# Second expert stage: sums kept in four banks over all experts, rows gathered per expert in float32, two more places for weights

## The chip, the cores and the metric

One Trainium2 chip, one of its cores. The metric is the device time of one execution in microseconds (us); lower is better. The kernel before was timed three times: 2516.45, 2519.05 and 2519.34 us, median 2519.05 us.

## What is computed

The program runs two transformer blocks of two layers each on 256 rows of 1024 floats. Each layer of the second block ends in a stage of 16 experts. In the first such stage two streams of 256 rows go through it (x and a context stream); in the second, which is the end of the program but for a last norm, only x does. What one stage computes, from the reference (`h` is the normalised and modulated x, `n` = 256, so each expert takes `cap` = 32 rows):

```python
def ec_moe(h, w_r, w1, w3, w2):
    cap = max(1, EC_CAPACITY * n // N_EXPERTS)
    aff = jax.nn.softmax((h @ w_r).astype(jnp.float32), axis=-1)
    gate, idx = lax.top_k(jnp.swapaxes(aff, 1, 2), cap)
    xin = jax.vmap(lambda hb, ib: hb[ib])(h, idx)
    hid = jax.nn.silu(jnp.einsum('becd,edf->becf', xin, w1)) * jnp.einsum('becd,edf->becf', xin, w3)
    ye = jnp.einsum('becf,efd->becd', hid, w2) * gate[..., None].astype(h.dtype)
    return jax.vmap(lambda yb, ib: jnp.zeros((n, D), h.dtype).at[ib.reshape(-1)].add(yb.reshape(-1, D)))(ye, idx)
...
        h2 = modulate(rmsnorm(x, g_norm2[i]), sh2, sc2)
        x = x + gt2 * ec_moe(h2, w_router[i], w_e1[i], w_e3[i], w_e2[i])
```

Every expert has three weight matrices of 1024 x 1024 floats (4 MiB each), so a stage reads 192 MiB.

## The kernel before

**The weights.** All large weights come through `Ring.load` and `Ring.load_pairs` (L137, L144): one DMA of 1 MiB on SP's queue into a tile of 8 KiB per partition. Such a tile is called a *place* here, and such a DMA a *load*. The ring hands the places out in a fixed order, so a load waits until the work that last used its place is done, and SP issues its DMAs strictly in order: a load that waits holds up all behind it. In the second expert stage, `moe(1, ...)`, the ring has 21 places (L1569 to L1572): two that are free from early on (`early`), one in `late`, the memory of the second half of the attention's normalised rows (`hp[1]`) at the ninth position, and 17 places `rE1_0` to `rE1_16` that lie where the attention stage had its own tiles and come free one by one as that stage ends. The memory of the first half of those normalised rows (`hp[0]`) is not a place: it takes the pieces that are gathered from. A stage makes 192 loads. One expert needs 12: four steps of the first product (`first_product`, L1610) with one load of `w_e1` and one of `w_e3` each, and four loads of `w_e2` for the second product.

**The start of the stage.** After the router's top-k (`topk`, L969) VectorE has the 16 x 32 row numbers. `u_onehot` (L989) spreads them over 128 partitions with one product on `ones16` and compares them with the row numbers, which gives the one-hot matrix `G` for all 16 experts (2 x 512 columns). `u_pieces` (L1005) splits the scaled rows into a high and a low float32r half (`hTh`, `hTl`), ScalarE writing one and VectorE the other. `u_gather` (L1039) then makes, for each of the eight blocks of 128 model columns, four products of 512 columns, and ScalarE or VectorE writes the result for all 16 experts at once into `xin` (16 KiB per partition), with the norm's scale and shift. Two blocks at a time are gathered ahead of each of the four steps of expert 0's first product (L1639 to L1648). Up to there the order of the instructions is as written (`tc.manual_schedule` from L1491 until `tail.close()`, L1650); behind it a scheduler sets the order on each engine.

**The loop over experts** (L1847 to L1855). Step e makes two steps of the first product of expert e, the whole `second_product` of expert e - 1, and the other two steps. `second_product` (L1783) turns the gated values (`gated`, L1774, into a tile `hd`) by four transposes, multiplies with `w_e2` into two banks `y`, scales by gate and output gate into `yg`, splits into `yh` and `yl` (`evac_hl`, L395) and sends the 32 rows back to their places among 256 by products with the one-hot `Se` (L1838, L1839), each 128 x 256 result in a bank of its own `b`; VectorE adds each to x (L1841).

PSUM has eight banks, all handed out by `bank` (L82). `gate_rows` (L538) prepares the output gate `gt` by two products of 512 columns (L543).

Of the kernel before, what the change touches and what calls it, by code (L numbers as in the profile page):

```python
# [69 lines left out]
def model(ctx, tc, I, out):  # L70
# [810 lines left out]
    RT = {}  # L881
# [107 lines left out]
    def u_onehot(s, bd, G):  # L989

        st = {}

        def spread():
            ixf = RT[s][1]
            d = bd()[0:16, 0:512].rearrange("p (e c) -> p e c", c=32)
            dve.tensor_tensor(d, ixf[:, None, :].to_broadcast([16, 16, 32]), ident[:16, :16, None].to_broadcast([16, 16, 32]),
                              op=ALU.mult)
            st["b"] = bank("b")
            pe.matmul(st["b"], ones16, d.rearrange("p e c -> p (e c)"), start=True, stop=True)

        def rows(t):
            return lambda: dve.tensor_scalar(G[:, t], st["b"], tokid[:, t:t + 1], None, op0=ALU.is_equal)
        return [spread, rows(0), rows(1)]
# [555 lines left out]
    def moe(l, ss, hp, sh, r, tail, ctx=None):  # L1559
# [3 lines left out]
        with ExitStack() as st:  # L1563
            if ns == 2:
                ring = Ring(st, f"rE{l}", 15, 0, [8, 9, 10, 11, 12, 13, 14, 0, 3, 1, 2, 4, 5, 6, 7])
                ring.ps.append(hp[1])
                ring.ps[0:0] = early
            else:
                ring = Ring(st, f"rE{l}", 17, 0, [0, 1, 2, 3, 4, 12, 13, 6, 5, 7, 8, 10, 9, 11, 14, 15, 16])  # L1569
                ring.ps[0:0] = [late]  # L1570
                ring.ps[6:6] = [hp[1]]
                ring.ps[0:0] = early  # L1572
            mo = opool(st, "mo", reuse_waits="tile")
            G = ns
            xin = mo.tile([128, 16 // G, 8, G, ns, 32], F32, name="xin")
            rg = mo.tile([128, 32], F32, name="rg")

# [5 lines left out]
            rp = opool(rst, "rt", reuse_waits="tile", side="right")  # L1583
# [25 lines left out]

            def first_product(hb, e, i):  # L1610
                if ns == 2:
                    return first_products(hb, e, i)
                t1, t3 = ld(I["w_e1_2"][l, e], i), ld(I["w_e3_2"][l, e], i)
                for kk in range(2):
                    k = 2 * i + kk
                    lhs = xin[:, e, k, 0, 0]
# [6 lines left out]
            xs, px, pl = u_pieces(0, r, hp)  # L1623
            xs["to"] = lambda c: xin[:, :, c, :, 0]
            gx, ex = u_gather(l, 0, xs, (dve, act))
            hb0 = [bank("h") for _ in range(4 if ns == 2 else 1)]
            if ns == 2:
# [3 lines left out]
            run(px[:2])  # L1631
            if ns == 2:
                run([ec[4], gc[6], ec[5], gc[7], ec[6], ec[7]])
            xs["G"] = (ctx["gp"] if ctx else rp).tile([128, 2, 512], F32R, name="G", tag="G")
            oh = u_onehot(0, lambda: per.tile([128, 512], F32R, name="bd", tag="mt", bufs=1), xs["G"])
            run([oh[0], pl[0], oh[1], pl[1], oh[2]])
            if ns == 2:
                sel(1)
            run([gx[0], gx[1], ex[0], ex[1]])  # L1639
            first_product(hb0, 0, 0)  # L1640
            run([gx[2], gx[3], ex[2], ex[3]])
            run(px[2:])
            run(pl[2:])
            first_product(hb0, 0, 1)
            run([gx[4], gx[5], ex[4], ex[5]])
            first_product(hb0, 0, 2)
            run([gx[6], gx[7], ex[6], ex[7]])
            first_product(hb0, 0, 3)  # L1648
# [15 lines left out]
            sh.close()  # L1664
            ap = opool(st, "ex", reuse_waits="tile")
            gt = ap.tile([128, D], F32, name="gt")

# [106 lines left out]
            def gated(e, hb):  # L1774

                hd = ap.tile([128, 512 * ns], F32, name="hd", tag="hd")
# [6 lines left out]
            def second_product(e, hd):  # L1783
# [59 lines left out]
            gate_rows(ap, gt, l, 1, rowsel, (lambda: per.tile([128, 512], F32, name="sel", tag="mt", bufs=1)) if ns == 2 else None)  # L1843
            if ns == 2:
                return pairs(hb0)
            hd = gated(0, hb0)
            for e in range(1, 16):  # L1847
# [3 lines left out]
                second_product(e - 1, hd)  # L1851
                first_product(hb, e, 2)
# [12 lines left out]
    moe(1, [0], hp, sh, r, tail)  # L1865
    sh1.close()
# [36 lines left out]
```

## Time and profile before

| what | us |
|---|---|
| three runs, median | 2519.05 |
| the profiled execution, its device time | 2521.02 |
| the profiled execution, its span (first to last instruction) | 2519.3 |
| TensorE busy, share of the span | 2365.8, 94% |
| chain that ended last: TensorE / DMA | 67% / 25% |
| mean granted TensorE clock | 0.987 of full |

The profiled execution took 2521.02 us, 1.97 above the median of the three runs; its span leaves out 1.7 us around the first and last instruction. The stage in question fills the end of the span, from about 2060 us on. In the page's forty slices the DMA's share is at nine tenths or more in the last slices and TensorE's digit falls to 7 and 8 there, while in the rest of the span it is the other way round. All times below are positions in this span.

### The profile page before, as it was taken

Reading aid. Unit: us, or ns where it says so; the run is one execution under the profiler, and the core shown is the slowest. Engines: PE = TensorE matmul, PEld = TensorE weight load, DVE = VectorE, ACT = ScalarE, POOL = GpSimd, SP = SyncE. Lnnn points to the kernel's source line nnn. Section 1 sums busy time; section 2 is a strip of 40 time slices with the busy share of each in tenths; the row PEclk is TensorE's granted clock in tenths of the full one; section 3 lists DMA queues with packets and bytes.
Section 4 is the critical chain, followed back from the end, with each engine's and each line's share of the span. In section 5 each row is a group of like instructions: output and inputs, shape, how many; then the busy total and the mean of one; then the engine's idle time right before and its main releaser. Section 6 shows DMA issues by size and latency. Waiting matters only on the chain.

```text
span 2519.3 us, 38429 instructions
## 1 busy us (share of the span) xinstructions
PE 2365.8 (94%) x15004; PEld 1709.6 (68%) x15004; DVE 1387.0 (55%) x2819; ACT 1062.8 (42%) x2152; POOL 134.4 (5%) x188
## 2 busy tenths in 40 slices
PE   8999999999999999999999999998999989778776
PEld 7788979788999999789843443447879973222222
DVE  5687665686867777987721111225688763222223
ACT  5765555465757656565420000005656532000001
POOL 0100000010000000100300000001010000000000
PEclk9999999999999999999999999998999989999999
DMA  7577565467654444746689999997674679999998
GB/s 272 217 258 261 184 218 175 160 243 272 215 150 152 163 168 168 220 151 231 245 359 427 427 426 427 427 416 248 189 232 148 226 307 398 427 426 427 427 427 347
DMA packets 274935, 709.11 MB, mean 281 GB/s; under 512 B 27135, under 2 KB 181489, under 8 KB 220994
## 3 DMA queue, kind: packets, MB, share of 16 engines
q1 hardware_dynamic: 274754, 706.66, 73.9%
q8 instruction: 118, 1.93, 0.3%
q14 instruction: 63, 0.52, 0.1%
HBM read 705.50 MB, written 1.12 MB: 280 GB/s over the span
## 4 chain that ended last, share of the span: by engine, by line
PE 67%; DMA 25%; DVE 5%; ACT 1%; issue 1%; POOL 0%; DVEq 0%; POOLq 0%; SPq 0%; ACTq 0%
DMA w<-in_w_e_dram 24%; PE b L86 13%; PE b L88 13%; PE b L87 13%; PE h L1607 5%; PE acc L86 3%; PE acc L87 3%; PE acc L88 3%; PE b L509 1%; PE b L1191 1%; PE y L1710 1%; DVE wl L161 1%; PE b L1048 1%; DMA w<-in_w_ada_dram 1%; PE o L1311 1%
## 5 line engine op out<-in xcount | busy, mean ns | idle before, releaser
L161 DVE TENSOR_TENSOR wl<-w,wh 128x512 fp32r<-128x512 f32 x896 | 600.8, 696 | 191.8 <-ACT wh L159 153.7
L159 ACT ACTIVATE wh<-w 128x512 fp32r<-128x512 f32 x896 | 531.6, 627 | 225.9 <-PE b L87 114.2
L86 PE MATMUL b<-hTh,wh 128*128 128x256 f32 x1584 | 453.6, 287 | 3.3 <-ACT hTh L386 2.1
L87 PE MATMUL b<-hTl,wh 128*128 128x256 f32 x1584 | 448.0, 283 | 2.2 <-DVE hTl L377 1.4
L88 PE MATMUL b<-hTh,wl 128*128 128x256 f32 x1584 | 448.4, 283 | 0.0
L86 PEld LDWEIGHTS b<-hTh,wh 128*128 128x128 f32 x1584 | 300.5, 190 | 15.5 <-issue 5.7
L87 PEld LDWEIGHTS b<-hTl,wh 128*128 128x128 f32 x1584 | 299.5, 189 | 5.2 <-DVE hTl L377 1.8
L88 PEld LDWEIGHTS b<-hTh,wl 128*128 128x128 f32 x1584 | 300.0, 189 | 0.3 <-DVE wl L161 0.3
L1607 PE MATMUL h<-w,xin 128*64 128x512 f32 x1024 | 255.9, 597 | 1.7 <-DMA w<-in_w_e_dram 1.7
L396 ACT ACTIVATE yh<-yg 128x256 fp32r<-128x256 f32 x96 | 39.1, 417 | 454.5 <-DVE yg L1831 267.8
L1607 PEld LDWEIGHTS h<-w,xin 128*64 128x64 f32 x1024 | 88.5, 137 | 146.0 <-issue 132.6
L1620 PE MATMUL h<-w,xin 128*32 128x512 f32 x512 | 163.3, 610 | 8.2 <-DMA w<-in_w_e_dram 7.1
L1831 DVE SCALAR_TENSOR_TENSOR yg<-y,rg,gt 128x256 f32<-128x256 f32 x64 | 28.1, 478 | 250.0 <-PE y L1800 249.8
L88 PE MATMUL b<-hT,wl 128*128 128x256 f32 x560 | 156.5, 279 | 0.2 <-DVE wl L161 0.2
L86 PE MATMUL b<-hT,wh 128*128 128x256 f32 x560 | 156.6, 280 | 0.1
L87 PE MATMUL b<-hT,wh 128*128 128x256 f32 x560 | 156.3, 279 | 0.0
L1800 PE MATMUL y<-w,hT 128*32 128x512 f32 (+1 forms) x544 | 129.9, 585 | 26.6 <-DMA w<-in_w_e_dram 26.2
L1621 PE MATMUL h<-w,xin 128*32 128x512 f32 x512 | 123.7, 610 | 21.9 <-DMA w<-in_w_e_dram 21.9
L1710 PE MATMUL y<-w,xin 128*64 128x512 f32 x448 | 111.6, 598 | 5.6 <-DMA w<-in_w_e_dram 5.6
L1800 PEld LDWEIGHTS y<-w,hT 128*32 128x32 f32 x544 | 30.3, 111 | 123.8 <-issue 68.8
L88 PEld LDWEIGHTS b<-hT,wl 128*128 128x128 f32 x560 | 105.2, 188 | 0.4 <-DVE wl L161 0.4
L86 PEld LDWEIGHTS b<-hT,wh 128*128 128x128 f32 x560 | 105.2, 188 | 0.3 <-ACT wh L159 0.3
(395 smaller groups left out, 4110.6 us busy)
## 6 DMA issues: line engine op xcount, KB each, us to landing
w<-in_w_e_dram SPq DMA_DIRECT2D x384, 1024.0 KB
w<-in_w_in_dram SPq DMA_DIRECT2D x92, 1024.0 KB
w<-in_w_ada_dram SPq DMA_DIRECT2D x48, 1024.0 KB
w<-in_ffn_w_up_dram SPq DMA_DIRECT2D x44, 1024.0 KB
w<-in_ffn_w_down_dram SPq DMA_DIRECT2D x22, 1024.0 KB
w<-in_dil_w_qkv_dram SPq DMA_DIRECT2D x18, 1024.0 KB
w<-in_w_branch_dram SPq DMA_DIRECT2D x18, 1024.0 KB
w<-in_sb_w_qkv_dram SPq DMA_DIRECT2D x12, 1024.0 KB
```

The costliest lines, as they stand in the source:

```text
L86: pe.matmul(o, s[0], m[0], start=start, stop=False, skip_group_check=True)
L87: pe.matmul(o, s[0], m[1], start=False, stop=False, skip_group_check=True)
L88: pe.matmul(o, s[1], m[0], start=False, stop=stop, skip_group_check=True)
L159: act.activation(hi, part, AF.Copy)
L161: dve.tensor_tensor(lo, part, hi.bitcast(F32), op=ALU.subtract)
L396: act.activation(hi, src, AF.Copy)
L1607: pe.matmul(hb[2 * j + n][64 * q:64 * q + 64], xin[:, p, k, q].rearrange("p s c -> p (s c)"), ts[j][q][:, kk, n * 512:n * 512 + 512], star ...
L1620: pe.matmul(hb[0][32 * n:32 * n + 32], lhs, t1[:, kk, ns_], **fl)
L1621: pe.matmul(hb[0][64 + 32 * n:96 + 32 * n], lhs, t3[:, kk, ns_], **fl)
L1710: pe.matmul(yb[p][cols.start // 512][64 * q:64 * q + 64, cols.start % 512:(cols.stop - 1) % 512 + 1], xin[:, p, k, :].rearrange("p q s c - ...
L1800: pe.matmul(yb[cols.start // 512][M * q:M * q + M, cols.start % 512:(cols.stop - 1) % 512 + 1], hT[:, k], w, start=kk == 0, stop=last, ski ...
L1831: dve.scalar_tensor_tensor(yg[:, c_], yb[n][:, c_], rg[:, 16 + e:17 + e], gt[:, xs_], op0=ALU.mult, op1=ALU.mult)
```

## The change

Only the second expert stage (`ns == 1`) is changed; up to its first instruction the order on every engine is the same as before.

- The rows are no longer scaled, split and gathered for all experts at once. `u_onehot` multiplies the comparison by the rows' norm factor as it writes the one-hot `G1` in float32, first for experts 0 and 1 (64 columns), later for the other 14 (448 columns). A new `taken(e, c)` makes, for one expert and one block c of model columns, two float32 products with 32 columns (the unchanged rows `xr` stationary, `G1` moving) into 32 columns of one bank, which ScalarE or VectorE moves into `xe` with scale and shift. Expert e + 1 is taken while expert e is worked on.
- The results are summed in four banks `acc` over all 16 experts, set to zero at the start by four products of 512 columns; x gets them after the last expert alone. The 120 additions to x of experts 0 to 14 go.
- `xin` goes (16 KiB), as does `hd` (now `gtr[0]`); `G1` and `xe` come. With that one more place `rE1_17` fits, and `hp[0]`, now unused in the stage, becomes a place too: 23 in place of 21, the new one `hpr` at the ninth position and `rE1_17` at the end.
- The small tiles of the start (`sel16`) lie on the other side of memory.

```diff
+        def spread(es=slice(0, 16)):
+            def f():
+                ixf, n = RT[s][1], es.stop - es.start
...
+                pe.matmul(st["b"][:, cs], ones16, st["d"][:, cs], start=True, stop=True, skip_group_check=True)
...
+                    dve.tensor_scalar(G[:, t, cs], st["b"][:, cs], tokid[:, t:t + 1], r[t], op0=ALU.is_equal, op1=ALU.mult)
...
+            return [u(slice(a, b)) for a, b in ((0, 2), (2, 16)) for u in (spread, lambda es: rows(0, es), lambda es: rows(1, es))]
...
-                ring = Ring(st, f"rE{l}", 17, 0, [0, 1, 2, 3, 4, 12, 13, 6, 5, 7, 8, 10, 9, 11, 14, 15, 16])
+                sh.close()
+                hp = (opool(sh, "hpr", reuse_waits="tile", side="right"), hp[1])
+                ring = Ring(st, f"rE{l}", 18, 0, [0, 1, 2, 3, 4, 12, 13, 6, 5, 7, 8, 10, 9, 11, 14, 15, 16, 17])
                 ring.ps[0:0] = [late]
-                ring.ps[6:6] = [hp[1]]
+                ring.ps[6:6] = [hp[0], hp[1]]
...
+            def taken(e, c):
+
+                if c == 0:
+                    xe[e] = mo.tile([128, 8, 32], F32, name="xe", tag="xe", bufs=2), bank("b")
+                to, b = xe[e][0][:, c], xe[e][1][:, 32 * c:32 * c + 32]
+                for t in range(2):
+                    pe.matmul(b, xr[:, t, pair(c)], G1[:, t, 32 * e:32 * e + 32], start=t == 0, stop=t == 1, skip_group_check=True)
+                scale, shift = Amod[l][0][1][:, c:c + 1], shiftcol(l, 0, 1, c)
+                if c % 2:
+                    act.activation(to, b, AF.Identity, scale=scale, bias=shift)
+                else:
+                    dve.tensor_scalar(to, b, scale, shift, op0=ALU.mult, op1=ALU.add)
...
+            def begin_one():
+                oh = u_onehot(0, bd, G1, r)
+                run(oh[:3])
+                for i in range(4):
+                    taken(0, 2 * i)
+                    taken(0, 2 * i + 1)
+                    first_product(hb0, 0, i)
+                    if i == 1:
+                        run(oh[3:])
...
-                        for s in reversed(ss):
-                            for t in range(2):
-                                b = bank("b")
-                                lhs = Se[:, s * 256 + t * 128:s * 256 + t * 128 + 128]
-                                pe.matmul(b[:, :256], lhs, yh, start=True, stop=False)
-                                pe.matmul(b[:, :256], lhs, yl, start=False, stop=True)
-                                x = X[s][:, t, xs_]
-                                dve.tensor_tensor(x, x, b[:, :256], op=ALU.add)
+                        for t in range(2):
+                            b = acc[t][n][:, c_]
+                            lhs = Se[:, t * 128:t * 128 + 128]
+                            pe.matmul(b, lhs, yh, start=False, stop=False, skip_group_check=True)
+                            pe.matmul(b, lhs, yl, start=False, stop=e == 15, skip_group_check=True)
+                            if e == 15:
+                                x = xr[:, t, xs_]
+                                dve.tensor_tensor(x, x, b, op=ALU.add)
...
+            zero = per.tile([128, 512], F32, name="zero", tag="mt", bufs=1)[:, 0:128]
+            dve.memset(zero, 0.0)
+            acc.extend([bank("acc") for _ in range(2)] for _ in range(2))
+            for t in range(2):
+                for n in range(2):
+                    pe.matmul(acc[t][n], zero, iota_f, start=True, stop=False, skip_group_check=True)
             hd = gated(0, hb0)
+            for c in range(8):
+                taken(1, c)
             for e in range(1, 16):
...
                 second_product(e - 1, hd)
+                if e < 15:
+                    for c in range(8):
+                        taken(e + 1, c)
```

**SP's queue, the end of the attention stage.** `w_out` is the attention's output matrix, `w_e_2` the experts' weights; in brackets what an issue waits for (a name with DMAHW is an earlier DMA). Before:

```order
L141 DMA w<-in_w_out_dram 128x2x1024 [waits DMAHW0_49,DVE_49]
L148 DMA w<-in_w_e_2_dram 128x2048 [waits PE_49]
L141 DMA w<-in_w_out_dram 128x2x1024 [waits DMAHW1_49,DVE_49]
L148 DMA w<-in_w_e_2_dram 128x2048 [waits DVE_49,PE_49]
L148 DMA w<-in_w_e_2_dram 128x2048 [waits DMAHW2_49]
L148 DMA w<-in_w_e_2_dram 128x2048 [waits DMAHW4_49,DMAHW3_49,DVE_49]
L148 DMA w<-in_w_e_2_dram 128x2048 [waits DMAHW6_49,DVE_49]
L148 DMA w<-in_w_e_2_dram 128x2048 [waits DMAHW5_49,DMAHW0_49,DVE_49]
L148 DMA w<-in_w_e_2_dram 128x2048 [waits PE_49]
```

and with the change:

```order
L141 DMA w<-in_w_out_dram 128x2x1024 [waits DMAHW0_49,DVE_49]
L148 DMA w<-in_w_e_2_dram 128x2048 [waits PE_49]
L141 DMA w<-in_w_out_dram 128x2x1024 [waits DMAHW1_49,DVE_49]
L148 DMA w<-in_w_e_2_dram 128x2048 [waits PE_49]
L148 DMA w<-in_w_e_2_dram 128x2048 [waits DMAHW2_49,DVE_49,PE_49]
L148 DMA w<-in_w_e_2_dram 128x2048 [waits DMAHW3_49]
L148 DMA w<-in_w_e_2_dram 128x2048 [waits DMAHW4_49,DVE_49]
L148 DMA w<-in_w_e_2_dram 128x2048 [waits DMAHW6_49,DMAHW5_49,DVE_49]
L148 DMA w<-in_w_e_2_dram 128x2048 [waits DMAHW0_49,DVE_49]
L148 DMA w<-in_w_e_2_dram 128x2048 [waits DMAHW7_49,PE_49]
```

The order of the DMAs is the same; from the second row on each load goes to the place that one load later had before, so one more load now stands ahead of the one that waits for TensorE alone (the last row of each).

**TensorE, the start of the stage** (`hTh`, `hTl` the pieces, `w` expert weights, `h` the first product's bank). Before:

```order
L999 MATMUL b<-bd,ones_5628 128x512 [waits DVE_49]
L1048 MATMUL b<-G,hTh 128x512 [waits DVE_49,Activation_49]
L1048 MATMUL b<-G,hTl 128x512
L1048 MATMUL b<-G,hTh 128x512 [waits DVE_49,Activation_49]
L1048 MATMUL b<-G,hTl 128x512
L1048 MATMUL b<-G,hTh 128x512 [waits PE_49]
L1048 MATMUL b<-G,hTl 128x512
L1048 MATMUL b<-G,hTh 128x512
L1048 MATMUL b<-G,hTl 128x512
L1620 MATMUL h<-w,xin 32x512 [waits DVE_49]
L1621 MATMUL h<-w,xin 32x512 [waits DMAHW4_49]
```

and with the change:

```order
L1003 MATMUL b<-bd,ones_5628 128x64 [waits DVE_49]
L1635 MATMUL b<-G_21431,xr 128x32 [waits DVE_49] x3
L1635 MATMUL b<-G_21431,xr 128x32
L1652 MATMUL h<-w,xe 32x512 [waits PE_49]
L1653 MATMUL h<-w,xe 32x512 [waits DMAHW4_49]
L1652 MATMUL h<-w,xe 32x512
L1653 MATMUL h<-w,xe 32x512
L1652 MATMUL h<-w,xe 32x512 [waits Activation_49]
...
L1700 MATMUL rg<-ident,sel_21435 128x16 [waits DVE_49]
L543 MATMUL b<-gtr_110,sel 128x512
L543 MATMUL b<-gtr_110,sel 128x512 [waits DVE_49]
L1899 MATMUL acc<-iota_f,zero 128x512 [waits DVE_49]
```

Eight wide products ahead of the first step have become four narrow ones. Three of these wait for VectorE: two for the two halves of `G1`, the third until VectorE has emptied the 32 columns that the first two filled. Behind the fourth step stand the four zeroing products.

**TensorE, an expert in the middle of the loop** (`y` the second product). Before:

```order
L1800 MATMUL y<-w,hT 32x512 [waits DMAHW4_49,Activation_49]
L1800 MATMUL y<-w,hT 32x512
L1800 MATMUL y<-w,hT 32x512 [waits DMAHW5_49]
L1800 MATMUL y<-w,hT 32x512
L1800 MATMUL y<-w,hT 32x512 [waits DMAHW6_49]
L1800 MATMUL y<-w,hT 32x512
```

and with the change:

```order
L1848 MATMUL y<-w,hT 32x512 [waits DMAHW0_49,Activation_49]
L1848 MATMUL y<-w,hT 32x512 [waits PE_49]
L1635 MATMUL b<-G_21431,xr 128x32 [waits PE_49]
L1635 MATMUL b<-G_21431,xr 128x32
L1635 MATMUL b<-G_21431,xr 128x32 [waits DVE_49]
L1635 MATMUL b<-G_21431,xr 128x32
L1635 MATMUL b<-G_21431,xr 128x32 [waits Activation_49]
L1635 MATMUL b<-G_21431,xr 128x32
L1848 MATMUL y<-w,hT 32x512 [waits DMAHW1_49]
```

The 16 products of the next expert's rows stand between the parts of the second product, and every second one waits for the engine that empties the columns before.

## Rows read from the trace of the kernel before

**Rows 1.** The profile's page: the span, and the DMA issues of the experts' weights

```profile
span 2519.3 us, 38429 instructions
...
w<-in_w_e_dram SPq DMA_DIRECT2D x384, 1024.0 KB
```

**Rows 2.** Busy time by stretches: stretch, length, each engine, granted clock, DMA share, GB/s

```profile
2140.00:2160.00 20.00, 14.97 (x86) 4.57 (x86) 3.34 (x9) 1.65 (x4) 0.00 (x0) 1.00 1.01 425
```

**Rows 3.** Who waited for whom, SP's queue, 2150 to 2500 us

```profile
SPq L148 <- DMA w<-in_w_e_dram: 275.0, 133, 3.1
```

**Rows 4.** The same stretches' view at the start of the stage

```profile
2052.00:2060.00 8.00, 7.79 (x55) 7.49 (x54) 3.13 (x7) 2.56 (x7) 1.15 (x3) 0.85 0.01 3
2068.00:2076.00 8.00, 2.64 (x5) 1.38 (x6) 6.80 (x20) 0.00 (x0) 0.00 (x0) 0.50 1.01 428
2076.00:2084.00 8.00, 8.00 (x46) 3.33 (x44) 1.90 (x3) 2.48 (x4) 0.00 (x0) 0.87 0.67 250
2084.00:2096.00 12.00, 11.49 (x68) 4.92 (x68) 4.43 (x11) 4.65 (x7) 0.00 (x0) 1.00 1.00 394
```

**Rows 5.** Timeline of SP's issues (start, length, queue, line, count), 2031 to 2098 us

```profile
2031.23 0.38 SPq L141 DMA_DIRECT2D w<-in_w_out_dram  x1
2037.50 0.80 SPq L148 DMA_DIRECT2D w<-in_w_e_dram  x2
2059.68 0.33 SPq L148 DMA_DIRECT2D w<-in_w_e_dram  x1
2080.24 0.80 SPq L148 DMA_DIRECT2D w<-in_w_e_dram  x2
2097.45 0.33 SPq L148 DMA_DIRECT2D w<-in_w_e_dram  x1
```

**Rows 6.** SP's waits, 2000 to 2110 us: total, times, longest

```profile
SPq L148 <- PE h L1621: 29.2, 6, 17.0
SPq L148 <- PE acc L88: 13.4, 1, 13.4
```

**Rows 7.** Timeline of the start: one-hot, gather, first step

```profile
2071.56 0.68 DVE L996 TENSOR_TENSOR bd<-ixf,ident 16x512 fp32r<-16x512 f32 x1
2072.29 0.79 PE L999 MATMUL b<-bd,ones 16*128 16x512 f32 x1 [5.97 <-DVE bd L996]
2073.12 0.75 DVE L1002 TENSOR_SCALAR G<-b,tokid 128x512 fp32r<-128x512 f32 x1 [0.22 <-PE b L999]
2078.13 0.62 PE L1620 MATMUL h<-w,xin 128*32 128x512 f32 x1
```

**Rows 8.** Timeline: the router's products, and two small moves

```profile
2055.30 1.96 PE L943 MATMUL b<-wra,P 128*128 128x16 f32 x16 [0.21 <-ACT P L932]
2090.45 0.21 DVE L1591 TENSOR_SCALAR sel<-ixf 16x128 f32<-16x128 f32 x1
2090.65 0.78 ACT L1056 ACTIVATE xin<-b,modT,A 128x512 f32<-128x512 f32 x1 [3.22 <-PE b L1048]
```

**Rows 9.** Timeline from the output gate to expert 0's second product

```profile
2093.17 1.28 ACT L1779 ACT_TABLE_LOAD   x1 [1.74 <-PE rg L1654]
...
2093.60 1.95 PE L543 MATMUL b<-gtr,sel 128*128 128x512 f32 x4 [0.51 <-DVE sel L1581]
...
2095.49 0.62 PE L1620 MATMUL h<-w,xin 128*32 128x512 f32 x1
...
2099.06 0.69 PE L1790 MATMUL b<-ident,hd 64*128 64x64 f32 x4
...
2100.22 3.93 PE L1800 MATMUL y<-w,hT 128*32 128x512 f32 x32
```

**Rows 10.** Groups by form, 2064 us to the end: products that send rows back

```profile
L1838 PE MATMUL b<-yh,Se 128*128 128x256 f32 x128 | 29.7, 308 | 15.7 <-ACT yh L396 15.7
L1839 PE MATMUL b<-yl,Se 128*128 128x256 f32 x128 | 29.3, 306 | 0.0
```

**Rows 11.** The chain that ended last, its last DMA piece (start, length)

```profile
2496.08 10.85 DMA w<-in_w_e_dram
```

More of the change, by code (lines that the diff above doesn't have):

```diff
@@ L987, in u_route, with u_onehot, rows, f @@
         return dict(prep=prep, sq=sq, tr=tr, logits=logits, soft=soft, turned=turned, rows=rows, topk=topk, r=st["r"])
-    def u_onehot(s, bd, G):
+    def u_onehot(s, bd, G, r=None):
         st = {}
[L993 to L1003, printed above, removed]
+        def spread(es=slice(0, 16)):
+            def f():
+                ixf, n = RT[s][1], es.stop - es.start
+                if "d" not in st:
+                    st["d"], st["b"] = bd()[0:16, 0:512], bank("b")
+                cs = slice(32 * es.start, 32 * es.stop)
+                d = st["d"][:, cs].rearrange("p (e c) -> p e c", c=32)
+                dve.tensor_tensor(d, ixf[:, None, :].to_broadcast([16, n, 32]), ident[:16, es, None].to_broadcast([16, n, 32]),
+                                  op=ALU.mult)
+                pe.matmul(st["b"][:, cs], ones16, st["d"][:, cs], start=True, stop=True, skip_group_check=True)
+            return f
+        def rows(t, es=slice(0, 16)):
+            def f():
+                cs = slice(32 * es.start, 32 * es.stop)
+                if r is None:
+                    dve.tensor_scalar(G[:, t, cs], st["b"][:, cs], tokid[:, t:t + 1], None, op0=ALU.is_equal)
+                else:
+                    dve.tensor_scalar(G[:, t, cs], st["b"][:, cs], tokid[:, t:t + 1], r[t], op0=ALU.is_equal, op1=ALU.mult)
+            return f
+        if r is not None:
+            return [u(slice(a, b)) for a, b in ((0, 2), (2, 16)) for u in (spread, lambda es: rows(0, es), lambda es: rows(1, es))]
+        return [spread(), rows(0), rows(1)]
     def u_pieces(s, r, hp, tmp=None):
@@ L1582, in moe @@
             rst = ExitStack()
-            rp = opool(rst, "rt", reuse_waits="tile", side="right")
+            rp = opool(rst, "rt", reuse_waits="tile", side=("left", "right")[ns - 1])
             sel16 = rp.tile([16, 2 * ns, rep, ns, 32], F32, name="sel16")
@@ L1621, in first_product, with begin @@
                         pe.matmul(hb[0][64 + 32 * n:96 + 32 * n], lhs, t3[:, kk, ns_], **fl)
-            xs, px, pl = u_pieces(0, r, hp)
-            xs["to"] = lambda c: xin[:, :, c, :, 0]
-            gx, ex = u_gather(l, 0, xs, (dve, act))
             hb0 = [bank("h") for _ in range(4 if ns == 2 else 1)]
-            if ns == 2:
+            bd = lambda: per.tile([128, 512], F32R, name="bd", tag="mt", bufs=1)
+            def begin():
+                xs, px, pl = u_pieces(0, r, hp)
+                xs["to"] = lambda c: xin[:, :, c, :, 0]
+                gx, ex = u_gather(l, 0, xs, (dve, act))
                 ctx["to"] = lambda c: xin[:, :, c, :, 1]
@@ L1630, in moe @@
                 run([u for c in range(2, 6) for u in (ec[c - 2], gc[c])])
-            run(px[:2])
-            if ns == 2:
[L1633 to L1648, printed above, removed]
+                run(px[:2])
+                run([ec[4], gc[6], ec[5], gc[7], ec[6], ec[7]])
+                xs["G"] = ctx["gp"].tile([128, 2, 512], F32R, name="G", tag="G")
+                oh = u_onehot(0, bd, xs["G"])
+                run([oh[0], pl[0], oh[1], pl[1], oh[2]])
+                sel(1)
+                run([gx[0], gx[1], ex[0], ex[1]])
+                first_product(hb0, 0, 0)
+                run([gx[2], gx[3], ex[2], ex[3]])
+                run(px[2:])
+                run(pl[2:])
+                first_product(hb0, 0, 1)
+                run([gx[4], gx[5], ex[4], ex[5]])
+                first_product(hb0, 0, 2)
+                run([gx[6], gx[7], ex[6], ex[7]])
+                first_product(hb0, 0, 3)
+            def begin_one():
[7 more added lines that the diff above has]
+                        run(oh[3:])
+            if ns == 2:
+                begin()
+            else:
+                begin_one()
             sel(0)
@@ L1865, in model @@
     moe(1, [0], hp, sh, r, tail)
+    sh.close()
     sh1.close()
```

18 lines of the change are left out of this document (12 added, 6 removed).

## The prediction, made before the changed kernel was run

> **What bounds the kernel now.** I read the page first: a load of expert weights is 1024 KB, and the span is 2519.3 us [rows 1]. Then the busy time by stretches in the middle of the second expert stage: the DMA share is 1.01 at 425 GB/s, while TensorE is busy for 14.97 of 20 us and VectorE for 3.34 [rows 2]. SP's waits there are for earlier DMAs, 275.0 us in 133 waits [rows 3], not for places. So the transfers set the pace: at 427 GB/s one load of 1.049 MB takes 2.46 us, the 12 of an expert 29.5 us. The chain ends the same way: its last long piece is a DMA of 10.85 us from 2496.08 on, landing at 2506.93 [rows 11]; 12.4 us of work follow. What the stage can gain is therefore the time in which the DMA engines stood idle before they ran without a break, so I looked there. From 2052 to 2060 they move 3 GB/s [rows 4]: SP waits 13.4 us for the last product of the attention's output [rows 6] and issues again at 2059.68 [rows 5]. From 2076 to 2084 they move 250 GB/s [rows 4]: all 21 places are full, and SP waits 17.0 us for expert 0's first step [rows 6], until 2080.24 [rows 5].
>
> How long an issue takes to bring data: seven loads go out from 2059.68 on (places 15 to 21). If data flow from 2061.35, they last 7 x 2.456 = 17.2 us, to 2078.55; 250 GB/s over 8 us means 8 x (1 - 250/427) = 3.3 us lost, so the flow resumes at about 2081.9, which is 1.65 us behind the issue at 2080.24. Both ends fit 1.65 us. From 2084 to 2096 another 12 x (1 - 394/427) = 0.9 us is lost, with only two to four loads in flight. In all 4.25 us.
>
> **The ninth place (`hpr`): -2.46 us.** Its load waits for the same products of the attention as the next one, and before that wait held nothing up: the place `hp[1]` took its load before the last `w_out` at 2031.23 [rows 5]. Now `hpr` takes that load, `hp[1]` the next at once behind 2031.23, and the load of 2037.50 is the one after. TensorE is busy almost throughout 2052 to 2060 [rows 4] and gets no `w_out` later, since the extra load stands behind the last of them in the queue. One load more has landed at 2059.68: 2.46 us. If `hpr` came free late, nothing.
>
> **The 23rd place and the earlier start: -4.25 us.** From 2059.68 eight loads go out instead of seven and last until 2061.35 + 19.65 = 2081.0. To leave no gap, the first step must free places by 2079.35. Its time, from rows: the row numbers are there at 2071.56 [rows 7]. Spreading 64 in place of 512 columns takes some 0.2 us (0.21 for 16x128 [rows 8]; 0.68 for 512 [rows 7]), the product on `ones16` 0.3 (0.79 for 512 columns), two pieces of `G1` 0.2 each (0.75 for 512 columns): 2072.5. A float32 product of `taken` consists of two records; the nearest row is the router's, 16 records of 128x16 in 1.96 us, 0.122 each [rows 8]. So `taken` costs four records, 0.49 us at the full clock, and 0.98 at the lower one of the two levels (1.2 GHz), which is granted here: 0.50 from 2068 to 2076 [rows 4]. Emptying 128x32 I put at 0.25 us with its signals (ends: 0.21 and 0.78 us [rows 8]; the size is nearer the first). Two `taken` with a wait between: 2074.75. Two steps of the first product run from 2095.49 to 2099.06, 1.75 us each [rows 9], 3.5 at the lower clock: the first step ends at 2078.2. That is 1.1 us early enough, and all of the 4.25 us go, if the refills that follow keep up.
>
> **The refills.** Each step frees two places, 4.9 us of transfer. At the full clock a step with two `taken` takes 0.49 + 0.4 + 0.49 + 1.75 = 3.1 us: second step at 2081.4. Ahead of the third VectorE writes the other 448 columns of `G1`, 0.4 + 2 x 0.67 us and then the emptying: third at 2085.6, fourth at 2088.8. Data then last until 2081.0 + 8 x 2.456 = 2100.7, without a gap. But behind the fourth step there is new work. The gate sum and the two `gate_rows` products end at 2091.4 (1.95 us for both [rows 9]); `zero` is set behind the table load (1.28 us [rows 9]) and expert 0's gating, 2092.0; four zeroing products at 0.9 to 0.98 us each [rows 9], 2095.6; two `taken` of expert 1 with their waits, 1.8 us; then expert 1's first step, which the order breaks into three parts with two `taken` between, 3.7 us: 2101.2. Before, that step ended at 2097.45 [rows 5], some five us behind the fourth one, which ends shortly ahead of the table load at 2093.17 [rows 9]; now it takes twelve. Needed by 2100.7 - 1.65 = 2099.05, it is 2.1 us late: **+2.1 us**. Running thin around it I put at half of the 0.9 us above: **+0.4**. Later refills are in time: `y` and its waits end near 2110.7, needed by 2111.
>
> **The loop.** An expert before: four steps at 1.75, transposes 0.69, second product 3.93 [rows 9], sending back (29.7 + 29.3)/16 = 3.7 us [rows 10], 15.3 in all. Added: 32 records at 0.122, 3.9 us, and eight waits of 0.35, 2.8 us: 22.0 of 29.5. The 7.5 us left cover it: 0. If that cover were gone each further us per expert would cost up to 15. The 120 additions taken from VectorE, and the 120 small moves given to it and to ScalarE, lie beside the transfers (VectorE is busy 3.34 of 20 us): 0, and below that only if a move held TensorE up by more than the waits counted. The wait for emptied columns is in the built order for every pair of products. The Trainium skill, PSUM — Partial Sum Buffer, section "PSUM bank collisions raise a hardware error", asks for just this, a guard by bank and not by address. Were the columns free of each other, the 2.8 us ahead of expert 1's step would go, and with them the late refill: 2512.9.
>
> **The end.** The last scatter of the second chunk must wait for the addition that reads its bank, +0.2 us behind the last load.
>
> **Sum:** -2.46 - 4.25 + 2.1 + 0.4 + 0.2 = -4.0 us. The profiled execution is 2521.02 us, 1.97 above the median of the three runs; the sum is a difference within that execution (it would be 2517.0), and I set it against the median: **2515.0 us**. 0.2% is 5.0 us, about what a measurement can tell from no change.
>
> **Rivals.**
> *No late refill.* The chain behind the fourth step is 2 us shorter (zeroing overlaps the gating, waits cost less). For it: the zeroing products need only VectorE's memset. Against: the order puts the memset behind the gating. -2.46 - 4.25 + 0.2 = -6.5: 2512.5.
> *Places that bring nothing.* `hpr` or `rE1_17` is still held when its turn comes (the latter waits for VectorE, ScalarE and TensorE), or emptying costs the 0.78 us of the far row: eight waits by 0.5 more make the refill 4 us later. Against: whatever lay in either place was read on the way to the row numbers, which are there at 2071.56 [rows 7]. Gain 0 to 1.5: 2518.
> *The clock, slower than before.* One mechanism: the start now is made of short products with waits between, and the granted clock, 0.50 there [rows 4], rises late. In the trace it had risen after some 4 us of wide products without waits (mean 0.87 in 2076 to 2084, 1.00 after [rows 4]). If it stayed at 0.50 until expert 1's first step, the work from 2078 on (four steps 7.0 us, ten `taken` 4.9, the gate 1.95, zeroing 3.6, in all 17.5) takes twice as long and the sum is -4.0 + 17.5 = +13.5: 2532.5. It decides from 4 us of extra work on, a quarter of that stretch. Against: from 2078 on steps of 1.75 us fill most of it. The Trainium skill, TensorE: Matmul & The Clock Gate, section "What's actually happening", says that the throttled state is the default and activity releases it, which is what makes the case possible.
> *TensorE as the bound*: 22.0 of 29.5 us speaks against it.
>
> **How the numbers follow.** Forecast 0.57, no late refill 0.23, places that bring nothing 0.12, clock 0.07, the rest 0.01. The forecast's own range is 2513 to 2517. Leaving out the clock and the outer ends, the range reaches from 2512.0 to 2519.5, which takes in the bounds of the emptying (0.21 and 0.78 us). Faster by over 0.2%, below 2514.0: the second case and a seventh of the first, 0.31. Slower: 0.08. The rest, 0.61.
>
> **What would show it.** Right: SP issues a load of expert weights right behind 2031.23, and eight between 2059.7 and 2063.5; DMA above 420 GB/s from 2061.4 to 2100, then one gap of about 2 us; first record of expert 0's first step near 2074.7; four zeroing products of 3.5 us in all; GB/s unchanged in the loop. Wrong: a gap before 2085 (start or places), a gap of over 4 us near 2100 (emptying, clock), SP in the loop waiting for TensorE, or a lower rate there.

## The result, and the profile after

| what | before | after |
|---|---|---|
| median, runs taken together (4 each), us | 2519.13 | 2552.05 |
| lowest to highest, us | 2516.45 to 2519.34 | 2550.16 to 2557.41 |
| span of the profiled execution, us | 2519.3 | 2552.1 |
| row numbers there (position in the span), us | 2071.36 | 2067.77 |
| from there to the end of the span, us | 447.9 | 484.3 |

Ratio after to before: 1.0137, 95% interval 1.0122 to 1.0152. The change costs 33 us; the forecast was 2515.0 with a range up to 2519.5. The fourth and fifth lines take out that an execution reaches the stage a few us earlier or later: from the row numbers on the loss is 36.4 us.

The page of the changed kernel, its span and its chain (before, TensorE had 67% of the chain and the DMAs 25%):

```profile
span 2552.1 us, 39545 instructions
...
PE 80%; DMA 11%; DVE 5%; ACT 2%; issue 1%; POOL 0%; SPq 0%; DVEq 0%; POOLq 0%; ACTq 0%
```

The stretches of the start, as in [rows 4] (stretch, length, TensorE, its weight loads, VectorE, ScalarE, GpSimd, granted clock, DMA share, GB/s):

```profile
2052.00:2060.00 8.00, 7.57 (x52) 7.12 (x51) 3.99 (x11) 4.18 (x11) 1.41 (x4) 0.79 0.36 121
...
2076.00:2084.00 8.00, 6.84 (x45) 2.83 (x45) 2.25 (x5) 0.76 (x2) 0.00 (x0) 0.84 1.01 427
2084.00:2096.00 12.00, 10.73 (x48) 4.75 (x44) 2.32 (x9) 3.45 (x5) 0.00 (x0) 0.96 1.02 425
2096.00:2104.00 8.00, 7.76 (x52) 3.50 (x52) 0.81 (x3) 1.14 (x3) 0.00 (x0) 1.00 0.39 135
```

and of the loop and the end:

```profile
2300.00:2320.00 20.00, 17.20 (x94) 8.04 (x96) 1.24 (x4) 1.90 (x5) 0.00 (x0) 0.84 1.01 426
...
2500.00:2520.00 20.00, 18.36 (x126) 6.53 (x122) 4.44 (x10) 2.59 (x6) 0.00 (x0) 0.88 0.52 184
2520.00:2540.00 20.00, 16.77 (x144) 7.35 (x134) 7.63 (x18) 3.98 (x10) 0.00 (x0) 0.91 0.08 27
```

The gap of 2076 to 2084 is gone, a larger one stands at 2096 to 2104, and the loop's transfers run at almost the old rate. They are through shortly before 2510, two or three us later than the 2506.93 of [rows 11]. But TensorE then works on for another 30 us. The time was lost behind the last load. SP's waits in the loop, as in [rows 3] (total, times, longest), say the same: they are now mostly for places, which TensorE frees; for earlier DMAs it waits 37.0 us in place of 275.0.

```profile
SPq L148 <- PE y L1848: 144.1, 21, 15.4
SPq L148 <- PE h L1653: 99.4, 40, 4.7
SPq L148 <- DMA w<-in_w_e_dram: 37.0, 23, 2.1
```

TensorE's waits in the same stretch, 2150 to 2500 us, before:

```profile
PE y L1800 <- DMA w<-in_w_e_dram: 25.3, 46, 0.8
PE h L1621 <- DMA w<-in_w_e_dram: 21.9, 24, 1.4
...
PE h L1620 <- DMA w<-in_w_e_dram: 7.1, 12, 1.2
```

and after:

```profile
PE b L1635 <- ACT xe L1638: 16.9, 36, 0.5
PE b L1635 <- DVE xe L1640: 16.3, 36, 0.5
PE b L1838 <- DVE gtr L1828: 15.9, 11, 1.4
```

Before, it waited 54.3 us for weights; now it waits for none, and 33.2 us for the moves that empty the 32 columns (L1635 is `taken`).

How far the work has come is read from one instruction that occurs once per expert, ScalarE's write of `hT` (start and length). Before, the first, fourth, 15th and 16th of 16:

```profile
2099.78 0.38 ACT L1795 ACTIVATE hT<-b 128x256 f32<-128x256 f32 x1 [3.59 <-PE b L1790]
...
2147.52 0.38 ACT L1795 ACTIVATE hT<-b 128x256 f32<-128x256 f32 x1 [1.51 <-PE b L1790]
...
2471.00 0.39 ACT L1795 ACTIVATE hT<-b 128x256 f32<-128x256 f32 x1 [1.51 <-PE b L1790]
2500.19 0.38 ACT L1795 ACTIVATE hT<-b 128x256 f32<-128x256 f32 x1 [1.28 <-PE b L1790]
```

and after, the first four and the last two:

```profile
2104.86 0.38 ACT L1843 ACTIVATE hT<-b 128x256 f32<-128x256 f32 x1 [1.23 <-PE b L1838]
2128.26 0.38 ACT L1843 ACTIVATE hT<-b 128x256 f32<-128x256 f32 x1 [1.23 <-PE b L1838]
2146.18 0.39 ACT L1843 ACTIVATE hT<-b 128x256 f32<-128x256 f32 x1 [1.23 <-PE b L1838]
2177.19 0.38 ACT L1843 ACTIVATE hT<-b 128x256 f32<-128x256 f32 x1 [1.50 <-PE b L1838]
...
2515.16 0.38 ACT L1843 ACTIVATE hT<-b 128x256 f32<-128x256 f32 x1 [1.51 <-PE b L1838]
2531.43 0.38 ACT L1843 ACTIVATE hT<-b 128x256 f32<-128x256 f32 x1 [1.28 <-PE b L1838]
```

Before, the first three experts take 47.7 us together (TensorE uses up the weights that had piled up in the places), then eleven take 323.5, 29.4 each: the pace of the transfers. After, the first three take 72.3 and the eleven 338.0, 30.7 each: TensorE never gets through the pile. What is left of it is worked off behind the last load. First write +5.1, three experts +24.6, eleven +14.5, the last one -12.9 (16.3 in place of 29.2, its weights are there), what follows +1.6: these are the 32.8 us between the two spans.

The first three experts after the change also show a contrast within one run. Two of them take 23.4 and 17.9 us at a granted clock of 1.00: there the built order has the gather's products among those of the first product, and TensorE waits for a move only once in each (0.21 us). In the third, 31.0 us at a mean of 0.89, five pieces of the gather stand in a row, each of the last four behind a wait of 0.47 us, and so it goes on in the loop.

Why 30.2 to 31.8 us per expert shows the timeline of TensorE's matmuls for one of them (start, length, line, tile, count, idle time and what ended it):

```profile
2330.22 0.69 PE L1838 MATMUL b<-ident,gtr 64*128 64x64 f32 x4 [1.45 <-DVE gtr L1828]
...
2333.89 1.45 PE L1848 MATMUL y<-w,hT 128*32 128x512 f32 x3
2335.27 0.66 PE L1635 MATMUL b<-G,xr 128*128 128x32 f32 x4
2336.33 0.66 PE L1635 MATMUL b<-G,xr 128*128 128x32 f32 x4 [0.41 <-DVE xe L1640]
...
2338.05 1.90 PE L1848 MATMUL y<-w,hT 128*32 128x512 f32 x4
...
2344.41 1.07 PE L1635 MATMUL b<-G,xr 128*128 128x32 f32 x4 [0.48 <-DVE xe L1640]
2345.40 6.45 PE L1848 MATMUL y<-w,hT 128*32 128x512 f32 x24
```

Each piece of four records of L1635 is one `taken` (two float32 products), 0.66 us, and in front of six of the eight stands a wait of 0.41 to 0.48. From 2344.4 on the records take 1.6 times as long and more: the granted clock has gone to its lower level (0.84 in 2300 to 2320, where it was 1.00 before), and the 24 records of the second product behind it take 6.45 us.

### The profile page after: what moved, and what is told of

Read it like the earlier page. It is cut to its first block, busy times and chain, and to the rows that moved or that the text cites. A ratio compares the mean times of both kernels' runs of the same rounds, so it can differ in the third digit from the quotient of the medians.

```text
span 2552.1 us, 39545 instructions
## 1 busy us (share of the span) xinstructions
PE 2418.8 (95%) x15493; PEld 1775.8 (70%) x15493; DVE 1362.9 (53%) x2759; ACT 1080.6 (42%) x2208; POOL 133.4 (5%) x188
## 4 chain that ended last, share of the span: by engine, by line
PE 80%; DMA 11%; DVE 5%; ACT 2%; issue 1%; POOL 0%; SPq 0%; DVEq 0%; POOLq 0%; ACTq 0%
PE b L86 13%; PE b L88 13%; PE b L87 13%; DMA w<-in_w_e_dram 10%; PE y L1848 4%; PE h L1624 4%; PE h L1653 4%; PE b L1635 3%; PE acc L86 3%; PE acc L87 3%; PE acc L88 3%; PE b L509 1%; PE h L1652 1%; PE b L1204 1%; PE y L1758 1%
## 5 line engine op out<-in xcount | busy, mean ns | idle before, releaser
L1652 PE MATMUL h<-w,xe 128*32 128x512 f32 x512 | 144.2, 632 | 0.0
L1848 PE MATMUL y<-w,hT 128*32 128x512 f32 (+1 forms) x544 | 138.2, 787 | 0.5 <-ACT hT L1843 0.5
L1635 PEld LDWEIGHTS b<-G,xr 128*128 128x128 f32 x512 | 77.5, 214 | 84.2 <-DVE xe L1640 31.7
L1653 PE MATMUL h<-w,xe 128*32 128x512 f32 x512 | 129.7, 632 | 0.0
L1635 PE MATMUL b<-G,xr 128*128 128x32 f32 x512 | 91.6, 305 | 37.3 <-DVE xe L1640 20.0
L1640 DVE TENSOR_SCALAR xe<-b,A,modT 128x32 f32<-128x32 f32 x64 | 19.8, 309 | 193.3 <-PE b L1635 193.0
L1638 ACT ACTIVATE xe<-b,modT,A 128x32 f32<-128x32 f32 x64 | 24.2, 378 | 216.3 <-PE b L1635 216.3
```

The costliest lines, as they stand in the source:

```text
L1635: pe.matmul(b, xr[:, t, pair(c)], G1[:, t, 32 * e:32 * e + 32], start=t == 0, stop=t == 1, skip_group_check=True)
L1848: pe.matmul(yb[cols.start // 512][M * q:M * q + M, cols.start % 512:(cols.stop - 1) % 512 + 1], hT[:, k], w, start=kk == 0, stop=last, ski ...
```

## The experiments

All ratios are against the kernel before on the same chip; differences between two experiments are given by the medians and, where they decide something, by the ratios. Three theories were told apart: W, the moves that stand between the gather's products, with the lower clock that follows, make TensorE the bound; N, the narrow float32 products alone do; B, the four banks held by the sums do.

**e1_batch.** All 16 products of an expert first, the eight moves behind them:

```diff
-                    for c in range(8):
-                        taken(e + 1, c)
+                    for part in range(2):
+                        for c in range(8):
+                            taken(e + 1, c, part)
```

(`part` 0 makes the products of block c, `part` 1 its move; expert 1 likewise.)

> Theory W (waits and clock): in the loop of the changed kernel an expert takes TensorE 30.2 to 31.8 us, more than the 29.5 of its transfers, because eight moves of 32 columns each hold up the next products (0.47 us six to eight times) and because the granted clock falls to the lower level behind them (24 records of the second product in 6.4 us). With all 16 products first and the eight moves behind them no product waits: some 25 us per expert, the transfers set the pace again, clock near 1.00 in the loop, SP waiting for DMAs, 2513 to 2520 us. Theory N (narrow products): the 32 float32 records of 32 columns are themselves too much, or lower the clock by themselves: clock still near 0.83 and 2540 to 2552 us. Theory B (banks): four banks held by the sums leave four for everything else, and that is what delays TensorE: 2540 us or more.

Measured: 2523.91 us, ratio 1.0019 (1.0009 to 1.0029). Waits of SP in 2150 to 2500 us, and TensorE's timeline of a gather:

```profile
SPq L148 <- DMA w<-in_w_e_dram: 277.8, 134, 3.4
```

```profile
2304.10 1.88 PE L1851 MATMUL y<-w,hT 128*32 128x512 f32 x4 [0.67 <-DMA w<-in_w_e_dram]
2305.91 3.96 PE L1636 MATMUL b<-G,xr 128*128 128x32 f32 x32
2309.80 5.30 PE L1851 MATMUL y<-w,hT 128*32 128x512 f32 x28
```

The gather takes 3.96 us instead of 8.3, the second product 7.2 instead of 9.1, SP waits for DMAs again, and 0.0118 of ratio, about 30 of the 33 us, are gone. W holds against N and B. But 2523.91 lies above the range given: the start (e3, e5) has its own loss.

**e2_pairs.** Two blocks' products, then their two moves beside each other, four times.

> Four products, then two moves beside each other, four times per expert: three or four waits in place of seven or eight. Theory W: some 28 us per expert even if the clock still falls, so the transfers set the pace: 2514 to 2523 us; if the clock is a matter of the waits' share it stands between 0.85 and 1.00 in the loop. Theory N: clock near 0.83, 2540 us or more. Theory B: 2540 us or more.

Measured: 2521.91 us, 1.0011 (1.0002 to 1.0021). TensorE's waits, 2150 to 2500 us:

```profile
PE b L1636 <- ACT xe L1641: 20.4, 24, 0.9
...
PE y L1851 <- DMA w<-in_w_e_dram: 4.9, 6, 2.0
...
PE h L1656 <- DMA w<-in_w_e_dram: 2.8, 4, 1.4
```

Two waits of 0.85 per expert stay. What an expert takes while the pile lasts, when TensorE waits for no weights, is its own pace: 21.4 to 23.0 us in e1_batch (`hT` from 2165.89 over 2188.93 to 2210.31), 27.1 in e2_pairs (from 2304.21 to 2331.31) and 30.2 to 31.8 in the changed kernel, against 29.5 of the transfers. For weights TensorE waits 36.0 us in all in e1_batch (20.2, 8.7 and 7.1), 7.7 in e2_pairs and none in the changed kernel; the first two sums understate the slack, because in part of the stretch TensorE still works off the pile. A few us per expert decide between nothing and 30 us in all. The granted clock is 0.91 to 1.00 over stretches of 60 us, within what was expected.

**e3_none.** No gather for experts 2 to 15:

```diff
-                if e < 15:
-                    for c in range(8):
-                        taken(e + 1, c)
...
-                    lhs = xe[e][0][:, k]
+                    lhs = xe[min(e, 1)][0][:, k]
```

> No rows are gathered for experts 2 to 15: they use those of expert 1 (left out: 14 of 16 gathers). What is left is the rest of the change: sums in four banks, 23 places, the new start. Theories W and N: the transfers set the pace, 2514 to 2520 us (start of the changed kernel's trace: 2.46 and 4.25 us gained, 5.5 and 1.0 us lost at 2096 to 2120). Theory B: still above 2530 us, since the banks are as before.

Measured: 2521.84 us, 1.0013 (1.0004 to 1.0023), just above the range. Sums in four banks, places and new start together are no gain, with the gather paid or not; B falls once more, and the forecast of -4.0 fails also without the loop.

**e4_batch_21.** As e1_batch, with `hpr` and `rE1_17` taken out of the ring.

> As e1_batch, with 21 places instead of 23. If the places are worth what the prediction put on them, slower than e1_batch by 2.5 (the ninth place alone) to 6.7 us; if nothing is gained by a place once the first step comes earlier than forecast, the same within 1 us. Theory N: TensorE sets the pace, and both are the same.

Measured: 2529.37 us, 1.0043 (1.0026 to 1.0060): 5.5 us slower than e1_batch by the medians, 6 by the ratios, with some 5 either way. In its trace the gap of 2076 to 2084 is back (291 GB/s; 413 in e1_batch). The two places are worth something; the size agrees with what was put on them, but the interval is too wide to confirm it.

**e5_nozero.** As e1_batch, without the zeroing:

```diff
-            for t in range(2):
-                for n in range(2):
-                    pe.matmul(acc[t][n], zero, iota_f, start=True, stop=False, skip_group_check=True)
...
-                            pe.matmul(b, lhs, yh, start=False, stop=False, skip_group_check=True)
+                            pe.matmul(b, lhs, yh, start=e == 0, stop=False, skip_group_check=True)
```

In this kernel, e6_first and e7_half a part of expert 0's result is left out of the sums (last section); no instruction is saved by that.

> e1_batch without the four zeroing products: the first expert's scatter starts each sum. In e1_batch's trace these products take TensorE 3.70 us just ahead of expert 1's gather and first step, while no place is free and the DMA engines run dry (369, 224 and 163 GB/s in 2084 to 2112, some 10 us of transfer lost). Theory Z (TensorE's chain up to expert 1's first steps sets when the transfers go on): the zeroing's 3.7 us come back one for one, 3 to 4 us faster than e1_batch, about 2520. Rival (the places or the clock of that stretch decide, the zeroing stands beside something else): within 1 us of e1_batch.

Measured: 2516.17 us, 0.9995 (0.9986 to 1.0004), 7.7 us below e1_batch. Stretches of e1_batch:

```profile
2096.00:2104.00 8.00, 7.55 (x44) 5.58 (x46) 0.33 (x2) 0.38 (x1) 0.00 (x0) 0.90 0.56 224
2104.00:2112.00 8.00, 8.00 (x48) 2.56 (x44) 0.91 (x3) 1.52 (x4) 0.00 (x0) 0.68 0.46 163
```

and of e5_nozero:

```profile
2096.00:2104.00 8.00, 8.00 (x65) 3.05 (x61) 0.62 (x2) 1.25 (x4) 0.00 (x0) 0.88 0.65 251
2104.00:2112.00 8.00, 8.00 (x67) 5.72 (x59) 3.73 (x9) 1.61 (x4) 0.00 (x0) 1.00 1.01 423
```

By the ratios it is 6 us, with some 3 either way: the zeroing stood on the path that sets the refills, as theory Z has it, and the rival falls. That more came back than its 3.7 us is not shown. In the two traces the granted clock differs already ahead of the zeroing, where the kernels are the same (0.50 and 0.63 in 2068 to 2076 and 2076 to 2084 of e1_batch, 0.62 and 0.80 of e5_nozero), so the stretches above hold that difference too, as well as the 0.68 behind the zeroing.

**e6_first** and **e7_half.** Expert 1's gather and first two steps ahead of the gate sum and the output gate; in e7_half only four of the eight blocks ahead, the other four behind the gates:

```diff
                 begin_one()
+                for part in range(2):
+                    for c in range(8):
+                        taken(1, c, part)
+                hb1 = [bank("h")]
+                first_product(hb1, 1, 0)
+                first_product(hb1, 1, 1)
```

> As e5_nozero, and expert 1's gather and its first two steps stand ahead of the gate sum and the output gate. Theory Z: the first refill behind expert 0's fourth step comes some 7 us earlier than in e1_batch (3.7 zeroing, about 3.4 gates), most of the 10 us lost at 2084 to 2112 comes back: 2513 to 2518 us, at or below the kernel before. Rival: the gates come later now, so expert 0's second product and its four places do, and the gap only moves to 2105 to 2115: 2518 to 2522.

> As e6_first, with half of expert 1's rows (four of eight blocks) ahead of its first two steps and the other half behind the gates: the refill another 2 us earlier. Theory Z: faster than e6_first by up to 2 us if a gap was left there, the same if not. Rival: the second half then stands between the gates and the second product, and nothing is gained.

Measured: 2516.05 us, 0.9996 (0.9987 to 1.0006), and 2513.84 us, 0.9990 (0.9980 to 1.0000). e6_first is no better than e5_nozero: in its trace the gap at 2096 to 2104 shrank (364 in place of 251 GB/s), but a second one stands at 2104 to 2112 (351), the rival's shift. By the ratios neither of the two can be told from e5_nozero, nor from each other. In e7_half's trace there is no gap left:

```profile
2096.00:2104.00 8.00, 8.00 (x60) 4.42 (x60) 2.23 (x6) 2.51 (x7) 0.00 (x0) 1.00 1.01 426
2104.00:2112.00 8.00, 8.00 (x68) 6.24 (x72) 2.74 (x8) 1.19 (x3) 0.00 (x0) 1.00 1.01 423
```

**e8_sums.** The kernel before, with the sums in four banks and their zeroing alone.

> The kernel before with one part of the change, the sums in four banks with their zeroing. The gather for all experts ahead of the loop and 21 places stay. In the loop TensorE waited some 4.7 us per expert for transfers, and VectorE was busy 3.3 of 20 us: nothing to gain there, 0. At the start 3.7 us of zeroing stand ahead of expert 1's steps. Theory Z: slower than the kernel before by 0 to 3.7 us, since its transfers were not dry in 2096 to 2120. Theory B (banks): slower by more, with TensorE waiting in the loop.

Measured: 2519.76 us, 1.0012 (1.0003 to 1.0022), 1.7 us slower by the medians, inside the range. The 120 additions taken from VectorE show no gain, as forecast.

**e9_filler.** The changed kernel, with work added where TensorE waits; the gather is also written ahead of the second product, no longer behind it:

```diff
+                        for c in range(8):
+                            taken(e + 1, c)
+                            pe.matmul(yb[c % 2][0:32, 0:256], ident[:, 0:32], iota_f[:, 0:256], start=True, stop=True,
+                                      skip_group_check=True)
```

> The changed kernel with work added: behind each of the eight pairs of gather products of an expert stands one more product of 32 x 256 whose result is overwritten (16 records more per expert, 8 x some 0.4 us), so that TensorE works where it stood still waiting for the move. Theory C (the clock that falls behind the waits is what tips TensorE over the pace of the transfers): no fall of the clock behind the gather, the second product back at the full clock, 3 us less per expert; faster than the changed kernel in spite of the added work, below 2535 us and granted clock over 0.93 in the loop. Theory D (the gather's length itself, products and waits, is enough, and the clock only follows): TensorE's time per expert the same or longer, clock near 0.83, 2545 us or more.

Measured: 2566.75 us, 1.0199 (1.0183 to 1.0215). Theory C's forecast fails. The waits for the moves fell from 33.2 to 9.5 us in 2150 to 2500, and from 2180 on the clock is 0.80 to 0.89 all the same; it falls earlier, in the gather itself:

```profile
2306.18 1.92 PE L1912 MATMUL y<-iota_f,ident 128*32 128x256 f32 x4
2308.02 1.07 PE L1635 MATMUL b<-G,xr 128*128 128x32 f32 x4
...
2322.70 4.05 PE L1849 MATMUL y<-w,hT 128*32 128x512 f32 x31
```

An expert then takes 30.5 to 33.9 us (the second product gains, 4.5 us in place of 9.1, and the added work takes it back), and some 8 us of transfer are lost at its start (11 GB/s in 2112 to 2120). So it is not standing still for the moves alone that brings the clock down. What does is open; e1_batch, where the clock averages 0.94 to 0.97, says only that a shorter gather costs less of it.

What e9_filler does not refute is that the clock decides. Its own second expert of the loop, from 2129.82 to 2153.97, ran at 1.00 and took 24.2 us; later ones with as many records (165) take 30.5 at a mean of 0.89, 32.2 at 0.84 and 33.8 at 0.80. By that one expert's pace, an estimate, TensorE at the full level would keep ahead of the 29.5 of the transfers even with all this work added. In the later experts the gather begins just behind a wait of 1.45 us for the gating, in the early one behind none; no run tests whether that matters.

**e10_best.** As e7_half, with `start=e == 0 and c == 0`.

> As e7_half, but a sum is started (first write instead of addition) only with the first half of its columns: the second half is then written by the first product that comes to it. Nothing of expert 0 is lost that way. Same instructions and same order as e7_half, so 2511 to 2516 us, 2 to 6 us below the kernel before.

Measured: 2514.00 us (11 runs; before 2517.95), 0.9987 (0.9978 to 0.9996): 4 us faster than the kernel before by the medians, 3.3 by the ratio (1.0 to 5.5). That is a version which keeps the change's places and sums and beats both kernels, by little.

## Why the prediction was wrong, step by step

**The loop: 0 was wrong, and it is nearly the whole error.** The step that failed is "22.0 of 29.5 us. The 7.5 us left cover it": an expert of the loop took 30.2 to 31.8 us. Two things were missing, the order in which the loop is built and the granted clock. The prediction's 3.93 us for the second product came from expert 0 [rows 9], whose four loads had all landed. In the loop the records come in pieces: four as each load comes, one after the other in one quarter of the columns. The kernel before, one expert of the loop:

```profile
2300.84 1.88 PE L1800 MATMUL y<-w,hT 128*32 128x512 f32 x4 [0.61 <-DMA w<-in_w_e_dram]
...
2305.65 1.90 PE L1800 MATMUL y<-w,hT 128*32 128x512 f32 x4 [0.54 <-DMA w<-in_w_e_dram]
2308.09 3.62 PE L1800 MATMUL y<-w,hT 128*32 128x512 f32 x20 [0.53 <-DMA w<-in_w_e_dram]
```

That is 9.3 us of work, and [rows 2], which the prediction quotes, warned of it: TensorE busy 14.97 of 20 us is 22.1 per expert, not 15.3. 15.3 fits an expert whose weights all lie there (the first three of the kernel before take 47.7 us, 15.9 each). With the added 6.7, 22.1 comes to 28.8 of 29.5, and any further us tips it. By parts, forecast and what the expert from 2323.09 to 2353.27 took (pieces of the chain of waits):

| part | forecast | measured |
|---|---|---|
| first product, 64 records | 7.0 | 8.15 |
| transposes, with the wait for the gating | 0.7 | 2.08 |
| second product | 3.9 | 9.07 |
| gather: products and waits | 6.7 | 8.30 |
| sending back | 3.7 | 2.57 |
| together | 22.0 | 30.17 |

In the second product some 3 us are the clock: 24 records take 6.45 us, where an expert of e1_batch at the full level makes 28 in 3.65:

```profile
2197.13 3.65 PE L1851 MATMUL y<-w,hT 128*32 128x512 f32 x28
```

The rest of its excess is the order, four and four records in 0.9 and 1.8 us between pieces of the gather. In the gather the waits were sized well (six of 0.46, 2.8), the records were not: 0.165 each instead of 0.122 and the last four at the lower clock, 5.5 in all. Without the clock's share, 2.8 us in the second product and 0.4 in the gather, the expert would take 27.0 us, an estimate from these rows: under 29.5, and what e2_pairs needs (27.1) without being slower than e1_batch. So the base and the gather's records used up most of the cover, and the lower clock, which the prediction priced for the start alone, took what was left. No run takes the clock away and leaves the waits, so this division is worked out and not shown; what e1_batch shows is that both go with the order of products and moves.

"If that cover were gone each further us per expert would cost up to 15" was also too small in kind: TensorE must not only keep the transfers' pace but also use up what 23 full places hold; it did not, and that alone was 24.6 us in three experts.

**The places: right, as far as the runs tell.** SP issues a load of expert weights at 2028.15, right behind the last `w_out`, and eight from 2056.10 on, as forecast. No gap before 2096, first step 3.78 us behind the row numbers (2071.55 less 2067.77; forecast 2074.75 less 2071.36, 3.4), and 5.5 us for the two places in e4_batch_21 against 6.7, with the wide interval given there.

**The late refill, +2.1: right in mechanism, too small.** SP issues at 2088.44 behind the fourth step, and again at 2101.07, with this between (timeline, all engines):

```profile
2088.87 1.12 PE L543 MATMUL b<-gtr,sel 128*128 128x512 f32 x2
...
2091.76 3.70 PE L1899 MATMUL acc<-iota_f,zero 128*128 128x512 f32 x8 [0.32 <-DVE zero L1895]
...
2095.29 0.55 PE L1635 MATMUL b<-G,xr 128*128 128x32 f32 x4
```

Both positions are the forecast's (2088.8 and 2101.2), but in this execution the stage began 3.6 us earlier, so TensorE was that much later than forecast, and the transfers were dry from about 2096 on: 8 x (1 - 135/427) = 5.5 us lost. Part of it is the clock: the third step, at 2081, again ran at the lower level, 3.4 us instead of 1.75. The rival on the clock named this place, with a larger price. In other executions more is lost there: in e1_batch's trace 8.7 us (224 and 163 GB/s), in e3_none's some 10.9 (345 GB/s in 2084 to 2096, 29 in 2096 to 2104, 403 and 391 in the next two stretches of 8 us), where the kernel before lost 4.25 in all. That eats the gain of the places, and e3_none stands at 1.0013 and not at the forecast.

**The chances.** The rival "TensorE as the bound" was dismissed in one line with 0.01, on the number that was wrong. The slack of 54.3 us in 350 of waits for weights, 4.6 us per expert, was there to be read, and 6.7 were to be added. It is a warning and no limit: e1_batch adds 3.96 us of gather and still waits 36.0 us for weights. The clock had a rival of its own (0.07), but at the start; none had it in the loop, where [rows 2] shows 1.00.

The Trainium skill, PSUM — Partial Sum Buffer, section "PSUM bank collisions raise a hardware error", whose waits the prediction counted in the loop and took as covered, bears on it after all: the guard by bank is what makes each `taken` wait for the move of other columns. e1_batch keeps the guard and takes away the waits by the order alone.

## What to carry to other kernels

A sum of durations taken where the data already lay is an engine's best case; its busy time in the stretch in question is the worse one. Here they were 15.3 and 22.1 us per expert. A forecast that hides new work should hold beside the larger of the two, and at the lower clock as well if the new work may bring it. Where products and moves alternate on one bank, make all products first and all moves behind. An engine that feeds back places must be faster than the transfers by enough to use up the pile at the start, or what is left of the pile is paid at the end.

## What the runs showed of the hardware

- A float32 product of 32 columns with 128 stationary ones costs 0.33 us in pairs between waits (0.66 for two), and 0.25 in a row of 16 (3.96 us).
- From 2180 on the granted clock falls to its lower level in each expert's gather of e9_filler, although TensorE is busy 54.75 of 60 us there (mean clock 0.89); between 2120 and 2180 it was 1.00 with 58.01 busy. The Trainium skill, TensorE: Matmul & The Clock Gate, section "What's actually happening", says that the throttled state is the default and that activity releases it; busy time in the profile did not tell here which level would be granted, and no run shows what does.
- A second start in one bank. With a start on both 256-column halves (e5 to e7) a part of expert 0's result is missing from the sums; with a start on the first half alone (e10_best) none is. That agrees with the Trainium skill, PSUM — Partial Sum Buffer, section "The four PSUM rules": a start clears the marks of the whole bank, so that the next addition to the other half overwrites it. The four zeroing products were a way round this that took 3.70 us on the path.
